# Modulation panels moved from mixer to feed-forward, silu by pairs, two squares summed by TensorE

## The chip, the cores and the metric

The kernel runs on one core of a Trainium2 chip. The metric is the device time of one execution in microseconds, the median of several runs. The engines are named as the profile names them: PE is TensorE (PEld its weight loads), DVE is VectorE, ACT is ScalarE, POOL is GpSimd, SP is SyncE, which issues the DMAs of the weights.

## What is computed

Two models follow each other on x, 256 tokens of width 1024 in fp32. The first is one layer of a delta rule and attention; the change touches it only in its norms. The second has two layers, and each of them is feed-forward, mixer, feed-forward. Every one of these has a norm in front that is modulated by a vector c: nine rows of 1024 per layer, each a product of silu(c) with 1024 columns of w_mod.

```python
for l in range(DEPTH_2):
    mod = silu(c) @ w_mod[l] + b_mod[l]
    sh1, sc1, g1, sh2, sc2, g2, sh3, sc3, g3 = split(mod[:, None, :], N_MOD)
    h = _rmsnorm_2(x) * (1.0 + sc1) + sh1
    x = x + HALF_STEP * g1 * _swiglu(h, ffn1_w_gate[l], ffn1_w_up[l], ffn1_w_down[l])
    h = _rmsnorm_2(x) * (1.0 + sc2) + sh2
    x = x + g2 * _hybrid_mixer(h, w_in[l], w_out[l], ...)
    h = _rmsnorm_2(x) * (1.0 + sc3) + sh3
    x = x + HALF_STEP * g3 * _swiglu(h, ffn2_w_gate[l], ffn2_w_up[l], ffn2_w_down[l])

def _swiglu(h, w_gate, w_up, w_down):            # 1024 -> 2816 -> 1024
    return (silu(h @ w_gate) * (h @ w_up)) @ w_down

def _hybrid_mixer(h, ...):                       # 28 panels of 128 columns of w_in
    qa, ka, va, qd, kd, vd, qh, fh, ih, gh = split(h @ w_in)
    o_a = stick_breaking(qa, ka, va)
    o_d = dilated_mixture(rope(norm(qd)), rope(norm(kd)), vd)
    o_h = hgrn2(silu(qh), gates(fh), ih)
    o_h = _rmsnorm_2(o_h) * hgrn_norm_g * silu(gh)
    return concat(o_a, o_d, o_h) @ w_out
```

## The kernel before

**Numbers.** All products are in fp32 by three matmuls: each operand is split into a rounded half H and a rest L, and L*H, H*H and H*L are added up (`mm3`). Weights come in panels of 128x1024. `wload` (L94) brings one: SP issues its DMA into a `raw` buffer (seven of them), ACT casts it to `wh` (L98), DVE subtracts to get `wl` (L99); of `wh` and `wl` there are four each. "Split" below means these two steps. Activations lie transposed, 128 channels by 256 tokens (T) in eight tiles (KD = 8).

**Stages.** First block to 372 us, feed-forward of layer 0 to 561, mixer to 716, feed-forward to 904, then layer 1 the same way: to 1092, 1247 and 1436. A feed-forward first runs 22 pairs f of a gate and an up panel (tiles `psf`, `psu`; 48 matmuls a pair), then eight panels m of the down matrix (`psd`).

**Order.** Code is written in the order of the mathematics; a scheduler then sets one fixed order for each engine's queue, by its own estimates of when things are ready. An engine works its queue strictly in that order.

**Norms.** `stat(k)` (L142) makes, for each eighth k of x, the scaled halves `xH` (ACT L152) and `xL` (DVE L153) and the square `sq` (ACT L155). The squares 1 to 6 are added to the first one, `sqa`, by POOL (L157, `tensor_add` on `seng`; by DVE in the first block's first two norms); the eighth, `sql`, is kept apart. `stat_close` (L160) has PE sum both over channels by a matmul with ones (`pss` L165, two matmuls for each tile, one for each half of the tokens), DVE adds the epsilon (`nms` L168), POOL takes the power (`nr` L170), PE spreads the result (`rb` L173). There are eight such norms. So that PE needn't wait for it, the first panels behind a norm are multiplied with the unnormed x (`pre`, L187: four panels in a mixer, five pairs in a feed-forward) and scaled afterwards; `norm` (L200) makes in the meantime the normed `hH` and `hL` (L206, L207) for the rest.

**Panels.** The modulation rows are computed by DVE: a panel of w_mod is loaded by SP, multiplied with silu(c) and summed by one instruction (L744, two records: the operation and the read of its sum). There are 8 panels to a row, 144 for both layers and 8 for the first block. `pump(n)` lets n of them run at that place of the program, `need(last)` drains what a stage's vector still lacks. `pump(1)` stands behind each f from `NPRE` on and behind seven of the eight m, and in the mixer behind each of the four dilated projections; `need(last)` stands at the end of the gate and up pairs, and in the mixer ahead of the output projection.

**Mixer.** Projections `pT` (one panel each, tile `psp`) and `ptok` (two panels, `pst`). After the four `pre` panels (gate f, `hsg`, `hk`, `hf`) come four for q (`hqt` by ACT L295, `hq` by DVE L296, from which the levels of the gated recurrence start: `RK`, `hs`), and so on. Interleaved generators make the stick-breaking part (`pv`), the dilated part (`nk`, `dk1a` on DVE L431, `dk1r` by POOL L432, `rp` L1204, `rsu`, `rke`, `rkb` L444; `ds`, `de`) and the recurrence (`hov`, sums of its squares `hjk` on ACT, `hra` DVE L431, `hrr` POOL L432, `hon` DVE L578, transposed by PE as `hot` L586, times the gate `hG` as `hy` L589, split as `yH`, `yL`). `hG` is the silu of four projections (L684); ACT keeps one set of function tables, and a change of set shows as ACT_TABLE_LOAD. Then come the output projections (`pso`) and `update`, which calls `stat` for the next norm.

## Time and profile before

| | us |
|---|---|
| median of 3 runs | 1442.99 (1441.73 to 1444.32) |
| the profiled execution, its own time | 1442.31 |
| its span, first to last instruction | 1440.5 |
| PE busy | 1403.3 (97%) |
| PEld busy | 1305.3 (91%) |
| DVE busy | 1141.0 (79%) |
| ACT busy | 771.0 (54%) |
| POOL busy | 85.7 (6%) |

Busy time is the union of an engine's instructions. Matmuls overlap: one of 256 columns is recorded with 0.28 us, but in a full stretch one starts every 0.12 us, so a wait is best read from the starts, or from the idle time in brackets behind a row, which names what ended it. "x4" behind a row counts records that follow each other; a pair of matmuls for `pss` leaves four. PEclk is the granted clock of TensorE, 1.00 for 2.4 GHz and 0.50 for 1.2 GHz.

### The profile page before, as it was taken

Reading aid. Unit: us, or ns where it says so; the run is one execution under the profiler, and the core shown is the slowest. Engines: PE = TensorE matmul, PEld = TensorE weight load, DVE = VectorE, ACT = ScalarE, POOL = GpSimd, SP = SyncE. Lnnn points to the kernel's source line nnn. Section 1 sums busy time; section 2 is a strip of 40 time slices with the busy share of each in tenths; the row PEclk is TensorE's granted clock in tenths of the full one; section 3 lists DMA queues with packets and bytes.
Section 4 is the critical chain, followed back from the end, with each engine's and each line's share of the span. In section 5 each row is a group of like instructions: output and inputs, shape, how many; then the busy total and the mean of one; then the engine's idle time right before and its main releaser. Section 6 shows DMA issues by size and latency. Waiting matters only on the chain. (4 is left out here: it accounts for less than half of the span.)

```text
span 1440.5 us, 27393 instructions
## 1 busy us (share of the span) xinstructions
PE 1403.3 (97%) x10786; PEld 1305.3 (91%) x10786; DVE 1141.0 (79%) x2124; ACT 771.0 (54%) x1315; POOL 85.7 (6%) x87
## 2 busy tenths in 40 slices
PE   7999989999999999999999999999999999999998
PEld 4798867889999989998899998999989998899997
DVE  6769888858887887888897797977688889796554
ACT  4654586644644446447564444544446357554442
POOL 0011100012100001001100001000011010100000
PEclk9999999999999999999999999999999999999999
DMA  8524545635688985557568897688774557577562
GB/s 317 195 64 124 150 147 174 222 103 164 198 288 276 323 286 182 176 153 252 171 202 303 271 356 243 201 283 286 237 255 158 172 175 234 175 242 241 172 199 70
DMA packets 94833, 303.98 MB, mean 211 GB/s; under 512 B 18128, under 2 KB 20432, under 8 KB 94448
## 3 DMA queue, kind: packets, MB, share of 16 engines
q1 hardware_dynamic: 89824, 299.90, 63.3%
q8 instruction: 85, 1.39, 0.4%
q10 hardware_dynamic: 4432, 1.11, 0.4%
q0 software_dynamic: 448, 1.21, 0.3%
q14 instruction: 44, 0.36, 0.1%
HBM read 300.09 MB, written 2.10 MB: 210 GB/s over the span
## 5 line engine op out<-in xcount | busy, mean ns | idle before, releaser
L98 ACT CAST wh<-raw 128x1024 fp32r<-128x1024 f32 (+3 forms) x407 | 414.6, 1021 | 288.2 <-PE psd L121 89.1
L99 DVE TENSOR_TENSOR wl<-raw,wh 128x1024 fp32r<-128x1024 f32 (+3 forms) x407 | 481.5, 1187 | 94.5 <-ACT wh L98 93.6
L111 PE MATMUL psf<-hH,wh 128*128 128x256 f32 x1088 | 306.1, 281 | 0.0
L112 PE MATMUL psf<-hL,wh 128*128 128x256 f32 x1088 | 305.6, 281 | 0.0
L110 PE MATMUL psf<-hH,wl 128*128 128x256 f32 x1088 | 305.4, 281 | 0.0
L121 PE MATMUL psd<-gHL,wh 128*128 128x512 f32 x704 | 244.3, 392 | 0.0
L744 DVE CUSTOM_DVE_ANT_0 raw<-raw,mrow 128x1024 f32<-128x1024 f32 x152 | 184.5, 1219 | 69.7 <-DMA raw<-in_wmod 68.1
L110 PEld LDWEIGHTS psf<-hH,wl 128*128 128x128 f32 x1088 | 205.6, 189 | 0.0
L112 PEld LDWEIGHTS psf<-hL,wh 128*128 128x128 f32 x1088 | 205.5, 189 | 0.0
L111 PEld LDWEIGHTS psf<-hH,wh 128*128 128x128 f32 x1088 | 204.8, 188 | 0.0
L122 PE MATMUL psd<-gHL,wl 128*128 128x256 f32 x704 | 196.8, 280 | 0.0
L121 PEld LDWEIGHTS psd<-gHL,wh 128*128 128x128 f32 x704 | 132.2, 188 | 29.0
L110 PE MATMUL psp<-hH,wl 128*128 128x256 f32 x512 | 149.6, 292 | 2.4 <-DVE wl L99 2.4
L111 PE MATMUL psp<-hH,wh 128*128 128x256 f32 x512 | 148.2, 289 | 0.0
L112 PE MATMUL psp<-hL,wh 128*128 128x256 f32 x512 | 147.0, 287 | 0.0
L122 PEld LDWEIGHTS psd<-gHL,wl 128*128 128x128 f32 x704 | 132.2, 188 | 0.0
L110 PEld LDWEIGHTS psp<-hH,wl 128*128 128x128 f32 x512 | 97.7, 191 | 5.5 <-PE psp L112 1.7
L112 PEld LDWEIGHTS psp<-hL,wh 128*128 128x128 f32 x512 | 97.7, 191 | 1.6 <-issue 1.0
L111 PEld LDWEIGHTS psp<-hH,wh 128*128 128x128 f32 x512 | 97.3, 190 | 1.2 <-issue 0.7
L249 ACT ACTIVATE ft<-psf 128x256 f32<-128x256 f32 x68 | 26.2, 386 | 112.2 <-PE psf L112 112.2
L157 POOL TENSOR_TENSOR sqa<-sqa,sq 128x256 f32<-128x256 f32 x36 | 31.3, 868 | 593.9 <-issue 481.3
L252 ACT CAST gHL<-ft 128x256 fp32r<-128x256 f32 x88 | 35.7, 406 | 28.1 <-DVE ft L250 22.3
(513 smaller groups left out, 2789.3 us busy)
## 6 DMA issues: line engine op xcount, KB each, us to landing
raw<-in_ffn_gu SPq DMA_DIRECT2D x176, 512.0 KB, 4.4
raw<-in_wmod SPq DMA_DIRECT2D x144, 512.0 KB, 4.5
raw<-in_ffn_dn SPq DMA_DIRECT2D x64, 448.0 KB, 4.1
raw<-in_win SPq DMA_DIRECT2D x56, 512.0 KB, 4.3
raw<-in_w_rest SPq DMA_DIRECT2D x32, 512.0 KB, 3.8
raw<-in_ffn_dn SPq DMA_DIRECT2D x32, 512.0 KB, 4.6
raw<-in_wmod_sc SPq DMA_DIRECT2D x12, 512.0 KB, 7.4
raw<-in_wout_a SPq DMA_DIRECT2D x16, 384.0 KB, 4.0
```

Of the source, the lines that this page charges most:

```text
L98: nc.scalar.copy(H[:, :n], raw[:, :n])
L99: nc.vector.tensor_sub(L[:, :n], raw[:, :n], H[:, :n].bitcast(F32))
L110: mm(ps, L[:, s], hH[:, b, :T], start=f, stop=False)
L111: mm(ps, H[:, s], hH[:, b, :T], start=False, stop=False)
L112: mm(ps, H[:, s], hL[:, b, :T], start=False, stop=l)
L121: mm(ps, H[:, s], h[:, b, :, :T], start=first and i == 0, stop=False)
L122: mm(ps[:, 1, :], L[:, s], h[:, b, 0, :T], start=False, stop=last and i == len(kw) - 1)
L157: self.seng.tensor_add(self.sqa, self.sqa, o)
L249: nc.scalar.activation(t, ps[:, 0, :], AF.Silu)
L252: nc.scalar.copy(gH[:, f, :], t)
L744: nc.vector.tensor_tensor_reduce(raw, raw, row, op0=ALU.mult, op1=ALU.add, scale=1.0, scalar=0.0, accum_out=t[:, j : j + 1])
```

## The change

1. `stat` and `stat_close`: the seventh square isn't added to `sqa` any more; both last squares stay apart, and PE sums three tiles instead of two.
2. `norm` takes a function that it calls ahead of its third and seventh step; the mixer gives it a `wload` of the next panel, and the first two `pT` behind it take these. The first four `wload` of a mixer stand ahead of its loop.
3. The four `pump(1)` of the mixer go; the feed-forward pumps two panels behind every third f and every second m.
4. The gate's projections are copied, and Silu runs once on each pair, 128x512.

```diff
-        if 0 < k < KD - 1:
+        if 0 < k < KD - 2:
             self.seng.tensor_add(self.sqa, self.sqa, o)
-        self.sql = o
+        elif k:
+            self.sql.append(o)
+        else:
+            self.sql = [o]
...
-        for i, a in enumerate((self.sqa, self.sql)):
+        for i, a in enumerate(self.sql):
             for t in range(2):
                 nc.tensor.matmul(pss[:, t : t + 1], a[:, t * P : (t + 1) * P], self.ones,
-                                 start=i == 0 and t == 0, stop=i == 1, skip_group_check=True)
+                                 start=i == 0 and t == 0, stop=i == 2, skip_group_check=True)
...
-    def norm(self, sh, into):
+    def norm(self, sh, into, between=None):
...
         for k in range(KD):
+            if between and k % 4 == 2:
+                between()
...
-                    self.pump(1)
+                    self.pump(1 + (f % 3 == 0))
...
-                self.pump(1 if m < 7 else 0)
+                self.pump(1 + m % 2 if m < 7 else 0)
...
-        self.mm3(ps[:, 0, :], self.wload(src), h, range(KD), range(KD), True, True)
+        self.mm3(ps[:, 0, :], src if isinstance(src, tuple) else self.wload(src), h, range(KD), range(KD), True, True)
...
-            pT = lambda: self.projT(win[next(u)], h)
+            Ws = [self.wload(win[next(u)]) for _ in range(4)]
+            ahead = []
+            pT = lambda: self.projT(win[next(u)] if not ahead else ahead.pop(0), h)
...
-                cz = self.pre(ps, self.wload(win[next(u)]))
+                cz = self.pre(ps, Ws[i])
...
-                    h = self.norm(sh, 0)
+                    h = self.norm(sh, 0, lambda: ahead.append(self.wload(win[next(u)])))
...
                 self.dil_q(pool, C, pT(), j, self.gq[:, l : l + 1], dz, nq)
                 next(st)
-                self.pump(1)
...
                 self.dil_k(pool, C, pT(), j, self.gk[:, l : l + 1], dT)
                 next(st)
-                self.pump(1)
...
-                nc.scalar.activation(G[:, i, :], z, AF.Silu)
+                nc.scalar.copy(G[:, i, :], z)
+                if i % 2:
+                    nc.scalar.activation(G[:, i - 1 : i + 1, :], G[:, i - 1 : i + 1, :], AF.Silu)
```

The lines of the kernel shift by 4 to 10 with the change (L99 stays, L157 becomes L161, L744 becomes L752). Three places show how the order of the engines moves.

DVE at the start of the first mixer, before: the eight steps of `hL`, then the split of the second `pT`'s panel, and the third's ahead of the second `hq`.

```order
L207 SCALAR_TENSOR_TENSOR hL_6557<-xs_6558,mod2_0_100,hH_6556 128x256 x8
L197 COPY cs_6449<-psp_6625 128x1
L640 TENSOR_TENSOR hsg_6659<-psp_6625,rbs_6462 128x256
L638 TENSOR_SCALAR hnz_6657<-cs_6449 128x1
L99 TENSOR_TENSOR wl_6703<-raw_6700,wh_6702 128x1024
L645 TENSOR_SCALAR hf_6464<-hsg_6619,lbq_4212 128x256
L296 SCALAR_TENSOR_TENSOR hq_6466<-hqt_6696,psp_6665 128x256
L645 TENSOR_SCALAR hf_6464<-hsg_6659,lbq_4212 128x256
L545 COPY RK_6863<-hf_6464 128x512
L522 TENSOR_TENSOR RK_6863<-hk_6465,RK_6863 128x256x2
L99 TENSOR_TENSOR wl_6737<-raw_6734,wh_6736 128x1024
L296 SCALAR_TENSOR_TENSOR hq_6466<-hqt_6730,psp_6699 128x256
```

After, behind the first six steps of `hL`: the split, two more steps, and the third panel's split behind the second `hq`.

```order
L201 COPY cs_6462<-psp_6658 128x1
L648 TENSOR_TENSOR hsg_6686<-psp_6658,rbs_6477 128x256
L646 TENSOR_SCALAR hnz_6684<-cs_6462 128x1
L99 TENSOR_TENSOR wl_6613<-raw_6610,wh_6612 128x1024
L213 SCALAR_TENSOR_TENSOR hL_6584<-xs_6585,mod2_0_100,hH_6583 128x256 x2
L653 TENSOR_SCALAR hf_6479<-hsg_6652,lbq_4213 128x256
L653 TENSOR_SCALAR hf_6479<-hsg_6686,lbq_4213 128x256
L302 SCALAR_TENSOR_TENSOR hq_6481<-hqt_6717,psp_6692 128x256
L551 COPY RK_6878<-hf_6479 128x512
L528 TENSOR_TENSOR RK_6878<-hk_6480,RK_6878 128x256x2
L302 SCALAR_TENSOR_TENSOR hq_6481<-hqt_6745,psp_6720 128x256
L99 TENSOR_TENSOR wl_6752<-raw_6749,wh_6751 128x1024
```

The third panel's `wl` has changed places with the second `hq`; two `hL` stand behind the second panel's `wl`.

DVE in the middle of the first mixer, from the first `dT` to the row behind `dk1a`, before: `dqa`, for which POOL then takes the power `dqr`, stands here, and so does DVE's use of `dqr`.

```order
L1207 TENSOR_TENSOR dT_6472<-rsu_7416 128x256
L431 TENSOR_SCALAR dqa_7623<-nq_6473 128x8
L744 ISA raw_7863,mcol_7355<-raw_7863,mrow_415 128x1024
L744 ISA mcol_7355 128x1
L446 TENSOR_TENSOR dT_6472<-dT_6472,rkb_7423 128x256
L451 TENSOR_SCALAR dqr_7624<-dqr_7624 128x8
L744 ISA raw_7866,mcol_7355<-raw_7866,mrow_415 128x1024
L744 ISA mcol_7355 128x1
L387 SCALAR_TENSOR_TENSOR sa_7433<-sa_7433 128x384
L387 SCALAR_TENSOR_TENSOR sa_7436<-sa_7436 128x384
L431 TENSOR_SCALAR dk1a_7496<-nk_7493 128x4
```

After, the same stretch: one panel is left in it, and `dqa` and `dqr` are gone from it (`dqa` now stands ten rows ahead of `dk0a`, `dqr` right behind that).

```order
L1215 TENSOR_TENSOR dT_6487<-rsu_7423 128x256
L752 ISA raw_7872,mcol_6308<-raw_7872,mrow_417 128x1024
L752 ISA mcol_6308 128x1
L452 TENSOR_TENSOR dT_6487<-dT_6487,rkb_7430 128x256
L393 SCALAR_TENSOR_TENSOR sa_7440<-sa_7440 128x384
L393 SCALAR_TENSOR_TENSOR sa_7443<-sa_7443 128x384
L437 TENSOR_SCALAR dk1a_7500<-nk_7497 128x4
```

Ahead of `dk1a` stand one panel and the two `dqa`, `dqr` rows fewer.

PE from the end of the first mixer to the feed-forward, before: the sum of `sqa`, then three matmuls on, that of the last square.

```order
L165 MATMUL pss_8263<-ones_88,sqa_8153 128x1 x2
L194 MATMUL psf_8277<-xL_8155,wh_8280 128x258
L194 MATMUL psf_8277<-xH_8154,wl_8281 128x258
L194 MATMUL psf_8277<-xH_8154,wh_8280 128x258
L165 MATMUL pss_8263<-ones_88,sq_8255 128x1 x2
L194 MATMUL psu_8291<-xH_8154,wh_8286 128x258
L194 MATMUL psf_8277<-xL_8155,wh_8280 128x258
L194 MATMUL psf_8277<-xH_8154,wl_8281 128x258
L194 MATMUL psf_8277<-xH_8154,wh_8280 128x258
L194 MATMUL psf_8277<-xL_8155,wh_8280 128x258
L194 MATMUL psu_8291<-xL_8155,wh_8286 128x258
L173 MATMUL rb_8272<-ident_86,nr_8270 128x128 x2
```

After, from the second of three sums on (the first one stands twelve matmuls ahead of it):

```order
L169 MATMUL pss_8268<-ones_88,sq_8256 128x1 x2
L198 MATMUL psf_8284<-xL_8161,wh_8287 128x258
L198 MATMUL psf_8284<-xH_8160,wl_8288 128x258
L198 MATMUL psf_8284<-xH_8160,wh_8287 128x258
L198 MATMUL psf_8284<-xL_8161,wh_8287 128x258
L198 MATMUL psf_8284<-xH_8160,wl_8288 128x258
L169 MATMUL pss_8268<-ones_88,sq_8260 128x1 x2
L198 MATMUL psf_8284<-xH_8160,wh_8287 128x258
L198 MATMUL psu_8298<-xH_8160,wh_8293 128x258
L198 MATMUL psf_8284<-xL_8161,wh_8287 128x258
L198 MATMUL psf_8284<-xH_8160,wl_8288 128x258
L198 MATMUL psf_8284<-xH_8160,wh_8287 128x258
```

The first sum has moved ahead by 15 matmuls of the feed-forward, the one of the seventh square is new, and `rb` follows the last sum at about the same distance.

## Rows read from the trace of the kernel before

**Rows 1.** The page's engines: busy us, share of the span, instructions

```profile
PE 1403.3 (97%) x10786; PEld 1305.3 (91%) x10786; DVE 1141.0 (79%) x2124; ACT 771.0 (54%) x1315; POOL 85.7 (6%) x87
```

**Rows 2.** Windows of feed-forward and mixer: engines, PEclk, DMA share, GB/s

```profile
400.00:500.00 100.00, 100.00 (x842) 100.00 (x841) 81.56 (x126) 47.59 (x71) 0.00 (x0) 1.00 0.85 295
...
561.00:716.00 155.00, 149.35 (x1207) 140.90 (x1206) 132.97 (x270) 90.75 (x156) 14.14 (x12) 1.00 0.57 185
```

**Rows 3.** PE's list of waits, whole span: us in total, times, longest

```profile
PE hot L586 <- DVE hon L578: 1.9, 2, 1.0
```

**Rows 4.** PE's timeline, first mixer's start: start, us; idle before in brackets

```profile
577.66 0.36 PE L110 MATMUL psp<-hH,wl 128*128 128x256 f32 x1 [0.65 <-DVE wl L99]
...
581.75 0.38 PE L110 MATMUL psp<-hH,wl 128*128 128x256 f32 x1 [0.56 <-DVE wl L99]
```

**Rows 5.** DVE's timeline of the same place

```profile
580.48 1.22 DVE L99 TENSOR_TENSOR wl<-raw,wh 128x1024 fp32r<-128x1024 f32 x1
581.62 0.41 DVE L296 SCALAR_TENSOR_TENSOR hq<-hqt,psp 128x256 f32<-128x256 f32 x1
```

**Rows 6.** PE's timeline, first mixer's middle

```profile
655.27 0.67 PE L1204 MATMUL rp<-rsu,Cdperm 128*128 128x256 f32 x2 [0.45 <-DVE dk1a L431]
...
657.84 0.71 PE L444 MATMUL rkb<-ident,rke 128*128 128x128 f32 x4 [0.73 <-DVE rsu L1205]
```

**Rows 7.** DVE's and POOL's timelines of the same place

```profile
652.81 0.17 DVE L451 TENSOR_SCALAR dqr<-dqr 128x8 f32<-128x8 f32 x1 [1.19 <-POOL dqr L432]
652.89 1.22 DVE L744 CUSTOM_DVE_ANT_0 raw<-raw,mrow 128x1024 f32<-128x1024 f32 x1
...
654.98 0.15 DVE L431 TENSOR_SCALAR dk1a<-nk 128x4 f32<-128x4 f32 x1
...
655.21 1.92 POOL L432 TENSOR_TENSOR dk1r<-dk1a,negh 128x4 f32<-128x4 f32 x1 [2.43 <-DVE dk1a L431]
```

**Rows 8.** PE's timeline, first mixer's tail

```profile
684.13 0.33 PE L586 MATMUL hot<-ident,hon 128*128 128x128 f32 x1 [0.96 <-DVE hon L578]
...
689.52 0.38 PE L110 MATMUL pso<-yH,wl 128*128 128x256 f32 x1 [0.34 <-ACT yH L289]
...
690.64 0.39 PE L112 MATMUL pso<-yL,wh 128*128 128x256 f32 x1 [0.39 <-DVE yL L290]
```

**Rows 9.** Window ahead of that tail, and DVE's row behind it

```profile
665.00:680.00 15.00, 15.00 (x130) 14.03 (x130) 15.00 (x43) 13.10 (x28) 0.00 (x0) 1.00 0.89 309
...
681.47 0.17 DVE L431 TENSOR_SCALAR hra<-hss 128x8 f32<-128x8 f32 x1 [0.15 <-ACT hjk L574]
```

**Rows 10.** ACT's table loads for the gate's silu

```profile
L684 ACT ACT_TABLE_LOAD x6 | 7.7, 1283 | 0.1
```

**Rows 11.** PE at the mixer's head and behind it; POOL's adds (page)

```profile
560.98 0.50 PE L165 MATMUL pss<-ones,sqa 128*128 128x1 f32 x4
561.34 0.37 PE L194 MATMUL psp<-xH,wl 128*128 128x258 f32 x1
...
719.34 0.61 PE L165 MATMUL pss<-ones,sqa 128*128 128x1 f32 x4 [0.72 <-POOL sqa L157]
...
L157 POOL TENSOR_TENSOR sqa<-sqa,sq 128x256 f32<-128x256 f32 x36 | 31.3, 868 | 593.9 <-issue 481.3
```

**Rows 12.** Panels: first mixer, then feed-forward

```profile
L744 DVE CUSTOM_DVE_ANT_0 raw<-raw,mrow x17: 1203/1216/1223, 598.4 to 677.2; 128x1024 f32<-128x1024 f32 x17
L744 DVE DVE_READ_ACCUMULATOR2_ANT mcol<- x17: 78/81/93, 599.5 to 678.4; 128x1 f32 x17
...
L744 DVE CUSTOM_DVE_ANT_0 raw<-raw,mrow 128x1024 f32<-128x1024 f32 x24 | 29.2, 1221 | 9.4 <-DMA raw<-in_wmod 9.4
```

**Rows 13.** Windows behind first and second mixer's end

```profile
723.00:725.00 2.00, 2.00 (x19) 2.00 (x19) 2.00 (x5) 1.73 (x2) 0.00 (x0) 1.00 0.10 20
1254.00:1256.00 2.00, 2.00 (x12) 2.00 (x11) 1.55 (x4) 1.14 (x2) 0.00 (x0) 0.50 0.22 16
```

**Rows 14.** The page's transfers in 40 slices

```profile
GB/s 317 195 64 124 150 147 174 222 103 164 198 288 276 323 286 182 176 153 252 171 202 303 271 356 243 201 283 286 237 255 158 172 175 234 175 242 241 172 199 70
```

## The prediction, as it was put on record

> **What bounds the kernel now.** I read the busy shares first, then the windows by stage, then PE's list of waits, and last the timelines around each wait. PE is busy for 97% of the span, and no other engine is close [rows 1]. In the feed-forward PE is busy for all of 100 us and issues 842 matmuls, one every 0.119 us [rows 2]: nothing on another engine can shorten that stage, it can only be harmed. In the mixer PE is busy 149.35 of 155 us [rows 2]. So what this change can win is PE's idle time in two mixers and at the norms, about 6 us each, and only where the moved work ends such a wait. The list of waits names them; the costliest that touch this change are hot on hon, psp on wl, and pss on the sums of squares [rows 3, 4, 11]. The second layer's mixer repeats the first's waits (hot has two, both alike, [rows 3]), so the rows are of the first and count twice.
>
> The sum is made against the profiled execution, 1442.31 us (span 1440.5), which is 0.7 us under the median of 1442.99; I apply the difference to the median.
>
> **Panels.** One panel costs DVE 1.22 us and a read of 0.08, 1.30 together [rows 12]. By the rule that what was not pumped is drained where the vector is needed, 17 panels stand in either mixer before [rows 12]; counted through the new pumps it is 14 in the first mixer and 5 in the second. DVE is thus freed of 3.9 and 15.6 us. None of that is on PE's path by itself: it counts only where DVE is what PE waits for.
>
> *Middle.* PE waits 0.45 us for rp and 0.73 for rkb [rows 6]. Behind both is dk1a on DVE at 654.98, queued behind a panel (652.89) and behind dqr, for which DVE stood 1.19 us waiting on POOL [rows 7]. In the new order dqa stands ten rows ahead of dk0a, so dqr is there before DVE comes to it, and dk1a no longer has that wait ahead of it. DVE could have it 1.2 us earlier. Then PE's own nk is late next: nk now stands 5 matmuls ahead of rp and rkb 11 behind it, 16 matmuls or 1.9 us and rp itself, which is about 0.2 us short of what POOL's power (1.92, [rows 7]) and the copies around it need. 1.18 less 0.18 gives **-1.0 us in each mixer** (0 to -1.2).
>
> *Tail.* DVE is busy for 15.00 of the 15 us up to 680 and ACT for 13.10 [rows 9]; hra follows at 681.47 [rows 9], and PE then waits 0.96 us for hot, 0.34 for yH and 0.39 for yL, 1.69 in all [rows 8]. In the second mixer only one panel stands between dT and hra, where some eleven stood, so hra loses up to 13 us of DVE work ahead of it and is bound by ACT and PE; PE's order has it transpose hon all four at once with 24 projection matmuls (2.9 us) behind it before ds. I take all 1.69, and 0.3 for two of the three refills (a first matmul behind a wait lasts about 0.1 longer than its neighbours): **-2.0 us** (-1.0 to -2.3). In the first mixer ten panels still stand ahead of hra, so DVE stays full there; it gains one split fewer ahead of hra and ACT's shorter chain. I take half of 1.69: **-0.85 us** (0 to -1.7).
>
> **Gate by pairs.** A table load is 1.28 us [rows 10]; loads fall from 11 to 7 in a mixer, 5.1 us of ACT, all near the tail, where ACT is 87% busy [rows 9]. The copies cost about what the four activations did. No wait of PE names hG, so this is worth only what it lets hov's squares, and with them hra, come earlier; that is in the tail's number, and nothing is added. A rule speaks against the pair: the Trainium skill, in "Perfetto Trace Analysis", section "Optimizing Scalar/DVE Operations", says that where ACT and DVE are not saturated but cause bubbles on others, breaking instructions up lets work finish sooner. Here both are nearly full just there [rows 9], so by the trace the condition isn't met; by the rule the pair would make hy later and the tail's 0.85 would shrink to nothing.
>
> **First weights ahead.** The first four splits stood in this order already, and only the two between the norm's steps are new: two hL now stand behind the second projection's split. PE waits 0.65 us for that split and 0.56 for the next [rows 4]. The first should fall to about 0.25. But the next split, which DVE started at 580.48 ahead of hq [rows 5], now stands behind hq, which itself needs the end of that projection and ACT's copy. That puts it at about 581.2, its end at 582.4, and PE's start 0.65 later than 581.75 [rows 4], with two more hs done meanwhile (0.3). Net **+0.3 us in each mixer** (-1.2 if nothing holds the split, +1.0 if the hs bring nothing and hL is late too).
>
> **Squares.** POOL loses one add of 0.87 us per norm [rows 11], PE gets a third pair of matmuls. A pair stands for 0.36 us on PE (560.98 to 561.34, [rows 11]). There are eight norms. At the heads of two mixers and of the second layer's first feed-forward PE didn't wait for the sum (the row at 560.98 has no idle before it), so it is **+0.36 us three times**. From mixer to feed-forward PE waited 0.72 [rows 11]; with the last add gone the sum is 1.1 us earlier, but PE's order puts that pair 15 matmuls earlier too, where it still waits about 0.5, and the short wait at rb behind it is covered: **-0.25 us twice** with the third pair paid (-0.7 to +0.4). From the first block to its feed-forward it is about +0.1. In the first block's head PE waits for other things at both norms; I take 0 (-0.5 to +0.7).
>
> **Feed-forward.** The panels' DMAs move with them, from a stage with a DMA share of 0.57 into one with 0.85 [rows 2]; SP issues win's panels in the order it had. The extra panels take DVE from 82% to 89% of the stage: one more per three pairs, which last 3 x 48 x 0.119 = 17.1 us. PE has no wait there, and I cost it at nothing. DVE's idle time is the cover; what happens when it is gone is the second rival.
>
> **Sum.** First mixer -1.0 - 0.85 + 0.3 + 0.36 - 0.25 = -1.4; second -1.0 - 2.0 + 0.3 + 0.36 - 0.25 = -2.6; the two other norms +0.5; first block 0. Together -3.5: 1438.8 for an execution such as the profiled one, **1439.5** as a median.
>
> **The clock.** At 1254 to 1256 the granted clock is 0.50 (1.2 GHz), and PE issued 12 matmuls where the first mixer's like stretch at full clock has 19 [rows 13]. That is some 0.8 us there, about 1.5 with the neighbouring slices. The work before it was the same in both layers. The Trainium skill, "TensorE: Matmul & The Clock Gate", section "What's actually happening", has the array at half clock by default and released by recent activity; by it, fewer waits should keep the drop away. The trace agrees that it comes behind waits, but the first layer had the same waits and no drop. I leave it out of the sum and in the range.
>
> **Rivals.** *Given back, no change (0.31).* The scheduler's new order hands out what the panels gave: rkb waits for nk, hra in the first mixer stays where it was behind ten panels, and hq holds the split for the whole +1.0. Then it is -0.5 in the first mixer's middle and tail, -1.5 in the second's, +2.0 at the two starts, +0.7 for the two mixers' head pairs, -0.5 behind them, +0.5 for the others: +0.7 or, with half of the start, -0.3, so 1442 to 1443.5. For it: DVE's order, which I can read; against: dqr's wait is plainly gone.
>
> *Slower: the feed-forward becomes DVE's (0.07).* DVE stood 9.4 us at 24 panels in 100 us, 0.39 each [rows 12]. At 89% busy its idle time is 1.85 us in 17.1, so four panels may wait 0.46 each; beyond that DVE runs late and PE stops at wl. At 0.60 it would be 0.56 us per 17.1, 4 us in a gate-and-up stage, 12 in the three that get more panels: 1451. The transfers would go from 295 GB/s at a share of 0.85 [rows 2] to 326 at 0.94. Against it: one slice of the page, 36 us in a feed-forward, moved 356 GB/s [rows 14] with PE full, and a wait of an engine that is early shrinks as it gets busier.
>
> *More (0.14).* The split isn't held (-1.2 instead of +0.3 in both mixers), or the first tail's waits go too (another -0.85) and the clock stays at 1.00 (-1.5): 1435.5 to 1437.2.
>
> *The panels don't leave the first mixer* is not a rival but a fact of the order, 14 of 17 stay; where a reader expects half the gain from there, it is missing.
>
> **How the numbers follow.** My forecast has 0.48, from about 1437.5 to 1441 by the bounds of middle, tail and start. About 0.2% is what a measurement of this kernel can tell from no change: below 1440.1 and above 1445.9. Of the forecast's 0.48, 0.43 lie below 1440.1, and all of "more"; that is 0.57 faster, 0.36 same, 0.07 slower. The range leaves out the slower rival, the upper part of "given back" and the lowest of "more": 1435.8 to 1443.2.
>
> **What would show it.** Right: no idle before rp, under 0.3 before rkb; in the second mixer's tail no idle before hot; the third projection's first matmul later by about 0.3 than before, counted from the second's start of norm; twelve records of pss in a norm instead of eight, 0.36 us more where PE doesn't wait; PE 100% in the feed-forward with DVE at 88 to 90%. Wrong: a wait on wl or on a panel in the feed-forward, a new drop of the granted clock, or hra unmoved in the second mixer.

## The result

The changed kernel takes 1461.96 us (median; 1460.51 to 1466.68) against 1443.47: a ratio of 1.0140, interval 1.0119 to 1.0161. It is slower by 18.5 us. The forecast was 1439.5 with a range to 1443.2, so the direction was wrong. What happened is the rival that had 0.07: in the feed-forward PE came to wait for DVE. A smaller loss, in the first block, was in none of the cases.

The page's engines of the changed kernel, as [rows 1], whose shares hardly move:

```profile
PE 1412.4 (97%) x10818; PEld 1309.5 (90%) x10818; DVE 1134.8 (78%) x2122; ACT 756.0 (52%) x1311; POOL 81.2 (6%) x81
```

The table is worked out from the traces: a stage lasts from PE's first matmul into `psf` or `psd`, or out of them into the mixer's tiles, to the next such matmul (the feed-forward's first matmuls that stand among a mixer's last ones count to the mixer). "gu" is a gate-and-up stage, "dn" the down stage behind it; 1.0 is the first feed-forward of layer 0, 2.0 the second, 1.1 and 2.1 those of layer 1. The kernels e1 to e20 are the experiments below.

```
            block1  gu1.0  dn1.0   mix0  gu2.0  dn2.0  gu1.1  dn1.1   mix1  gu2.1
before      372.99 126.98  61.38 155.09 126.35  61.38 126.69  61.38 155.13 127.88
after       377.00 132.37  64.60 155.63 126.69  62.95 131.48  64.46 151.89 126.37
e1 panels   373.31 132.66  63.56 154.31 126.82  64.16 132.11  62.85 154.89 126.35
e2 no pan.  379.42 126.83  61.83 156.72 126.34  61.83 126.84  63.32 155.62 126.38
e3 squares  379.54 126.85  61.83 155.25 126.33  61.83 126.83  61.83 155.29 126.37
e5          377.44 126.83  61.83 158.61 126.38  61.83 126.84  62.80 159.87 126.35
e6          377.94 128.97  62.44 153.48 129.53  63.66 128.84  62.96 151.71 126.35
e7          407.72 128.78  61.83 157.94 126.36  61.83 126.83  61.83 151.52 126.36
e12         372.58 131.15  64.04 154.83 127.47  63.47 131.95  62.90 151.77 126.33
e13         372.04 128.78  64.64 152.54 126.33  62.97 130.58  62.15 151.77 126.33
e14         377.51 127.05  61.83 155.39 126.38  61.83 126.81  63.27 155.06 126.38
e15         371.56 127.19  61.38 156.20 126.35  61.38 126.70  61.39 156.40 127.79
e16         371.39 127.18  61.38 154.85 126.96  64.37 126.71  62.16 154.70 126.34
e17         371.64 127.05  61.83 155.22 126.38  61.83 126.82  61.83 155.34 126.37
e20         372.80 127.19  61.38 152.52 128.36  61.38 126.70  61.91 152.80 126.34
```

After less before: first block +4.0; the three feed-forwards that got doubled pumps +8.6, +1.9 and +7.9; first mixer +0.5, second -3.2; the last gate-and-up stage -1.5.

PE's list of waits in the changed kernel has two lines that before has not, both in the feed-forward:

```profile
PE psf L110 <- DVE ft L256: 6.5, 5, 1.9
...
PE psd L122 <- DVE wl L99: 4.5, 6, 1.4
```

A window of 100 us of the first feed-forward, and one of the second mixer, as [rows 2]; the columns are PE, PEld, DVE, ACT and POOL busy, PEclk, DMA share, GB/s:

```profile
400.00:500.00 100.00, 97.38 (x813) 96.76 (x813) 78.95 (x125) 43.98 (x67) 0.00 (x0) 1.00 0.85 289
1115.00:1267.00 152.00, 147.66 (x1207) 140.66 (x1208) 120.13 (x245) 86.58 (x154) 13.89 (x13) 1.00 0.47 147
```

PE issues 813 matmuls where it issued 842, and DVE is less busy than before (78.95 against 81.56), not more. The panels' row for the same 100 us, as the last of [rows 12], tells why:

```profile
L752 DVE CUSTOM_DVE_ANT_0 raw<-raw,mrow 128x1024 f32<-128x1024 f32 x24 | 29.3, 1221 | 19.5 <-DMA raw<-in_wmod 19.5
```

As many panels, 24, of the same 1221 ns; but DVE stood 19.5 us waiting for their transfers instead of 9.4. One such wait in full, first SP's issue of the panel, then DVE from the panel before it on, then PE:

```profile
496.74 0.33 SPq L90 DMA_DIRECT2D raw<-in_wmod  x1
```

```profile
495.49 1.22 DVE L752 CUSTOM_DVE_ANT_0 raw<-raw,mrow 128x1024 f32<-128x1024 f32 x1
496.63 0.08 DVE L752 DVE_READ_ACCUMULATOR2_ANT mcol<- 128x1 f32 x1
...
498.18 1.22 DVE L99 TENSOR_TENSOR wl<-raw,wh 128x1024 fp32r<-128x1024 f32 x1
501.92 1.23 DVE L752 CUSTOM_DVE_ANT_0 raw<-raw,mrow 128x1024 f32<-128x1024 f32 x1 [2.52 <-DMA raw<-in_wmod]
503.07 0.08 DVE L752 DVE_READ_ACCUMULATOR2_ANT mcol<- 128x1 f32 x1
503.07 0.42 DVE L256 TENSOR_TENSOR ft<-ft,psf 128x256 f32<-128x256 f32 x1
```

```profile
503.54 0.39 PE L110 MATMUL psf<-hH,wl 128*128 128x256 f32 x1 [1.93 <-DVE ft L256]
```

DVE has read the sum of the panel before at 496.71 (496.63 and 0.08); the next panel's transfer is issued at 496.74, right behind that. DVE comes to it at 499.4 and stands until 501.92. Behind it in DVE's queue is `ft`, which empties a buffer of `psf`; PE stands 1.93 us for that buffer and starts 0.05 after `ft` ends. It is the rival's chain, a late DVE, but for its end: the rival had PE stop at `wl`, and in this stage PE stops at `ft`.

### The profile page after: what moved, and what is told of

Its sections match the earlier page's. It is cut to its first block, busy times and chain, and to the rows that moved or that the text cites. A ratio compares the mean times of both kernels' runs of the same rounds, so it can differ in the third digit from the quotient of the medians.

```text
span 1458.7 us, 27446 instructions
## 1 busy us (share of the span) xinstructions
PE 1412.4 (97%) x10818; PEld 1309.5 (90%) x10818; DVE 1134.8 (78%) x2122; ACT 756.0 (52%) x1311; POOL 81.2 (6%) x81
## 5 line engine op out<-in xcount | busy, mean ns | idle before, releaser
L99 DVE TENSOR_TENSOR wl<-raw,wh 128x1024 fp32r<-128x1024 f32 (+3 forms) x407 | 481.2, 1186 | 86.4 <-ACT wh L98 85.3
L752 DVE CUSTOM_DVE_ANT_0 raw<-raw,mrow 128x1024 f32<-128x1024 f32 x152 | 185.2, 1220 | 91.1 <-DMA raw<-in_wmod 89.6
L152 ACT ACTIVATE xH<-xT,mod 128x256 fp32r<-128x256 f32 x48 | 24.4, 508 | 77.8 <-DVE xT L219 77.4
```

The lines of the kernel that those rows point to most:

```text
L99: nc.vector.tensor_sub(L[:, :n], raw[:, :n], H[:, :n].bitcast(F32))
L152: nc.scalar.activation(H, x, AF.Copy, scale=s)
L752: nc.vector.tensor_tensor_reduce(raw, raw, row, op0=ALU.mult, op1=ALU.add, scale=1.0, scalar=0.0, accum_out=t[:, j : j + 1])
```

## The experiments

### Which edit: panels alone, everything but the panels, mixer's pumps away alone

e1 is the kernel before with

```diff
-                    self.pump(1)
+                    self.pump(1 + (f % 3 == 0))
-                self.pump(1 if m < 7 else 0)
+                self.pump(1 + m % 2 if m < 7 else 0)
-                self.pump(1)     # behind dil_q and behind dil_k
```

> The kernel before with the change's pumps alone (none in the mixer, two behind every third f and every second m); squares, norm and gate as before. DVE's order in the first feed-forward is then that of the changed kernel. Theory A (a panel whose transfer is late stands in DVE's queue ahead of ft and wl, and PE stops behind it; the pumps alone bring that order): the three feed-forwards with double pumps lose about what they lost in the changed kernel, +8.7, +1.9 and +7.9 us, the second mixer gains about 3, the first block stays at 373 us: 1455 to 1460. Theory B (the third pair of sums or the other edits disturb the feed-forward): near 1440. The first block's +4 us is from the sum of squares by both.

Measured 1458.96 (ratio 1.0119, 1.0103 to 1.0135). PE's list of waits of e1 has the same two lines:

```profile
PE psf L110 <- DVE ft L250: 6.7, 7, 1.4
...
PE psd L122 <- DVE wl L99: 4.1, 5, 1.2
```

Feed-forwards +18.0 in sum, the first block at 373.3. So the pumps alone bring the feed-forward's loss. The second mixer missed: 154.89, though it holds 5 panels as in the changed kernel.

e2 is the changed kernel with these lines put back.

> The changed kernel with all pumps as before: squares, weights ahead and gate by pairs stay. Theory A: no wait of PE on ft or wl in the feed-forwards, whose lengths are those of before (127 and 61 us); the first block is 4 us longer as in the changed kernel, the mixers lose or gain under 2 us: 1443 to 1448. Theory B: the feed-forwards still lose over 10 us in sum, 1455 or more.

Measured 1450.65 (1.0061, 1.0043 to 1.0079), a little above the range: the first block lost 6.4 and not 4, the first mixer 1.6, and the down stages 2.8 in sum. All gate-and-up stages are those of before.

e5 puts back the feed-forward's two lines only.

> The changed kernel with the feed-forward's pumps as before; the mixer's four pumps stay away, so its panels are drained ahead of the output projection. Theory A: the feed-forwards are those of before; the first block +4, mixers near those of the kernel without the panels' edit, 1440 to 1448. If leaving the pumps out of the mixer is what harms (its drain at the end), a mixer is longer by over 2 us than with pumps.

Measured 1455.33 (1.0090, 1.0071 to 1.0109), above the range: the mixers take 158.6 and 159.9, where e2 with its pumps takes 156.7 and 155.6. PE waits 9.3 us there for the output projection's `wl`: what is not pumped is drained by `need(last)` ahead of those splits on DVE, all 17 at once. So pumps may leave the mixer only as far as panels leave it.

### What about them: DVE's work, the transfer, the ring, or the place

e7 leaves the transfers out and keeps the work:

```diff
-            raw = self.wraw(src, 1024)
-            nc.vector.tensor_tensor_reduce(raw, raw, row, ...)
+            raw = self.stand                  # one standing buffer; weights keep six
+            nc.vector.tensor_tensor_reduce(raw, row, row, ...)
```

> The changed kernel with the panels' transfers left out: DVE runs the panel's instruction as often and for as long, on data that stand in its memory (the modulation is then not that of the reference), and the weights keep six raw buffers. Theory A (DVE's instructions fit; the late transfer ahead of ft and wl is what stops PE): no wait of PE on ft or wl in the feed-forwards, which take 127 and 61 to 62 us; with the first block's 4 and the second mixer's gain 1440 to 1445. Theory A2 (the instructions themselves are too many for DVE where two stand together): PE's waits on ft stay, the three feed-forwards lose over 10 us in sum: 1453 or more.

The total (1478.53, 1.0250, 1.0218 to 1.0281) is far above the theory's range and says nothing here: with nothing to wait for, the scheduler put 78 panels into the first block, which grew to 407.7 us. But its first feed-forward then holds 44 panels where the others hold 25, and 22 in its down stage. The windows of both, and the panels' row of the first:

```profile
408.00:536.00 128.00, 126.57 (x1060) 126.16 (x1059) 126.28 (x221) 65.18 (x99) 1.64 (x1) 1.00 0.59 178
536.00:598.00 62.00, 62.00 (x364) 54.69 (x362) 61.97 (x96) 29.69 (x41) 3.97 (x6) 1.00 0.60 182
```

```profile
L754 DVE CUSTOM_DVE_ANT_0 praw<-mrow 128x1024 f32<-128x1024 f32 x44 | 55.1, 1253 | 0.0
```

Forty-four panels without a wait cost that stage 1.8 us: DVE is busy 126.28 of 128, so it is just the bound, and 22 in the down stage cost nothing beside the third sum (61.83 is also e3's). The scheduler placed them, more than two to a pair where the pumps stand. In the changed kernel 25 with late transfers cost 5.4. DVE's work is not what was too much.

e6 halves the transfers: every second panel reuses the buffer of the one ahead of it.

```diff
-            raw = self.wraw(src, 1024)
+            if j % 2 == 0:
+                raw = self.wraw(src, 1024)
```

> The changed kernel, but every second panel is not loaded: the instruction runs a second time on the buffer of the panel before it, so DVE does the same work with half the panels' transfers and buffers (the modulation is then made from half of its columns). Theory A1 (what is late is the transfer, because the panel takes a place in the ring of seven raw buffers and is issued only when a slot comes free): PE's waits on ft and wl in the feed-forward go, the three feed-forwards come back to within 1 us of before in sum: 1441 to 1447 with the first block's 4 us. Theory A2 (DVE itself is overloaded where two panels stand together, 2 x 1.30 us ahead of ft): they stay, over 10 us: 1455 or more.

Measured 1453.40 (1.0075, 1.0047 to 1.0103), between the two. Window and panels' row of the first feed-forward:

```profile
400.00:500.00 100.00, 98.36 (x823) 97.95 (x822) 80.50 (x130) 45.44 (x69) 0.00 (x0) 1.00 0.73 237
```

```profile
L753 DVE CUSTOM_DVE_ANT_0 raw<-raw,mrow 128x1024 f32<-128x1024 f32 x25 | 30.6, 1222 | 17.7 <-DMA raw<-in_wmod 17.7
```

Moving 237 instead of 289 GB/s DVE still waits 17.7 us, on half as many transfers. So it isn't the traffic that makes a panel late. My A1 said that halving would do; it did only in part (128.97 us for this stage, and 129.53 for the second one). I read it so that a panel that stands early in DVE's queue waits for its own transfer however few others there are; no run tests that alone.

e8 gives the panels two raw buffers of their own and the weights five (`wraw(src, 1024, "praw", 2)`).

> The changed kernel with two raw buffers for the panels alone and five for the weights, seven in all as before. If the panels are late because they share one ring with the weights (a panel's transfer can be issued only when the load seven places before it has been split), the panels' waits on DVE fall to under half (89.6 us before) and the three feed-forwards come back to within 4 us in sum: 1442 to 1450. If they are late because DVE's order puts the panel ahead of weights that SP issues first, its waits stay near 90 us and so does the loss of 18: 1455 to 1465.

Measured 1491.39 (1.0358, 1.0320 to 1.0396), outside both: with five buffers the first block alone takes 403.8 us and the first mixer 169.3. Whether a larger ring would cure the lateness stays open; none was tried.

e14 is the changed kernel with the gate-and-up loop's pump as before; the down stage keeps its doubled pumps.

```diff
-                    self.pump(1 + (f % 3 == 0))
+                    self.pump(1)
```

> The changed kernel with one pump behind every f as before; the down phase keeps two behind every second m, the mixer none. The gate-and-up stages then hold as many panels as before and as after (24 to 25 in the first, drained at its end), only their places differ. Theory (two panels side by side in DVE's queue, with late transfers, stop PE; not their number in the stage): the first gate-and-up stage takes 126.8 instead of 132.4 us, the down stages still lose 1.5 to 3 each: 1446 to 1454, more where the mixer has to drain what the feed-forward did not take. Rival (their number decides): 132 us in the first gate-and-up stage.

Measured 1448.55 (1.0038, 1.0023 to 1.0054), as the theory had it, but the down stages lose less than it said (0.45, 0.45 and 1.9): most of what they lose in the changed kernel also comes from the doubled pumps ahead of them. Windows of the first feed-forward's two stages, and the panels' row as above:

```profile
377.50:504.50 127.00, 127.00 (x1066) 127.00 (x1066) 104.03 (x177) 65.43 (x99) 0.72 (x1) 1.00 0.79 268
504.50:566.50 62.00, 62.00 (x363) 54.70 (x363) 51.97 (x71) 30.88 (x41) 5.09 (x6) 1.00 0.89 300
```

```profile
L752 DVE CUSTOM_DVE_ANT_0 raw<-raw,mrow 128x1024 f32<-128x1024 f32 x23 | 28.0, 1222 | 18.8 <-DMA raw<-in_wmod 18.8
```

PE stands nowhere, with 25 panels in the stage as in both other kernels and 9 in the down stage as in the changed one. DVE waits 18.8 us for transfers here too, almost as long as in the changed kernel. So neither the number of panels nor the sum of the waits decides. e3 (below), whose pumps are those of before, says the same: its stage takes 126.85 us with this row, where before's waits are 9.4 in all:

```profile
L747 DVE CUSTOM_DVE_ANT_0 raw<-raw,mrow 128x1024 f32<-128x1024 f32 x24 | 29.2, 1224 | 19.9 <-DMA raw<-in_wmod 19.9
```

What decides is the place together with the waits: late transfers cost nothing behind single pumps (e14, e3), and work side by side costs little without transfers (e7). A sum that fits is that of one pair's 5.7 us. By the starts of e14's rows (441.30 to 445.47), a pair with one panel is 4.2 us of DVE's work (two splits, a panel and two small operations), which leaves 1.5 for a wait, and e14's waits are 1.0 to 1.8; with two it is 5.4, which leaves 0.3, and what a wait takes beyond that goes to PE. This is an estimate: taken over three pairs (13.8 of 17.1 us, 0.8 left for each of four panels) it fits as well, and no run tells the two apart. In before and in e14 the panels that are left over are drained at the end of the stage, when the pairs' own weights have landed.

### Squares

e3 is the kernel before with the change to `stat` and `stat_close` alone.

> The kernel before with the change to the squares alone. Theory (the four to six us that the first block lost come from its head, where the third pair of sums and two squares kept apart reorder PE and DVE and the clock falls at 20 to 40 us): the first block takes 377 to 379 us instead of 373, the granted clock is under 1.00 between 20 and 40 us, each mixer's and the second layer's head 0.4 us longer: 1446 to 1450. Rival (the first block's loss comes from the gate, the norm or chance): first block at 373, 1442 to 1444.

Measured 1447.79 (1.0044, 1.0028 to 1.0060). PE's rows in the first block's head, before and then e3:

```profile
28.14 2.32 PE L967 MATMUL psm<-raw,cc 128*2 128x256 f32 x10
31.99 0.58 PE L165 MATMUL pss<-ones,sqa 128*128 128x1 f32 x4 [1.53 <-DVE sqa L157]
```

```profile
28.65 0.59 PE L970 MATMUL psm<-raw,cc 128*2 128x256 f32 x2
31.02 0.58 PE L168 MATMUL pss<-ones,sqa 128*128 128x1 f32 x4 [1.78 <-DVE sqa L157]
...
31.97 0.59 PE L970 MATMUL psm<-raw,cc 128*2 128x256 f32 x2
32.50 0.95 PE L168 MATMUL pss<-ones,sq 128*128 128x1 f32 x4
33.38 1.87 PE L970 MATMUL psm<-raw,cc 128*2 128x256 f32 x4
```

Before, ten matmuls of the first modulation (`psm`) stand ahead of the second norm's sum; now two do, and the rest wait behind sums and `rb` for DVE's squares. Their raw buffers come free later: from 24 to 48 us SP waits 19.3 us for `psm` in e3, 13.2 in before, and the DMA share at 36 to 40 falls from 0.93 to 0.56, in these windows of before and of e3 (the last three columns are PEclk, DMA share, GB/s):

```profile
32.00:36.00 4.00, 4.00 (x24) 2.32 (x25) 2.81 (x8) 0.56 (x2) 1.26 (x2) 1.00 0.88 264
36.00:40.00 4.00, 4.00 (x21) 1.57 (x20) 3.17 (x9) 3.86 (x10) 0.02 (x1) 1.00 0.93 358
```

```profile
32.00:36.00 4.00, 3.85 (x14) 1.88 (x14) 1.31 (x5) 0.00 (x0) 1.61 (x1) 0.57 0.83 246
36.00:40.00 4.00, 4.00 (x13) 1.42 (x13) 2.55 (x5) 1.22 (x3) 0.40 (x1) 0.57 0.56 158
```

The clock falls too, to 0.57, and that has a price of its own: 12 matmuls of `psm` take 4.15 us, where before 18 take 4.05, some 1.4 us by that rate (an estimate).

```profile
35.71 4.05 PE L967 MATMUL psm<-raw,cc 128*2 128x256 f32 x18
```

```profile
36.54 4.15 PE L970 MATMUL psm<-raw,cc 128*2 128x256 f32 x12
```

How much of the head's loss is the clock and how much the order was not separated. A smaller drop need not cost in the end: e12, the changed kernel without the squares, has one in these windows, is 1.4 us late at `psb`'s first matmul (44.3 us in before; e3 is 4.3 late there), and its first block still takes 372.6 us.

```profile
32.00:36.00 4.00, 4.00 (x20) 2.25 (x20) 2.15 (x7) 0.36 (x1) 1.28 (x2) 0.75 0.89 256
36.00:40.00 4.00, 4.00 (x18) 1.52 (x17) 3.34 (x9) 2.98 (x7) 0.00 (x0) 0.82 0.67 256
```

> The changed kernel with the squares as before. Theory (squares cost the first block 4 to 6 us and each norm 0.36 where PE doesn't wait; panels cost the feed-forwards 18): the first block is back at 373, the feed-forwards stay slow (132, 64, 127, 63, 131, 64), the second mixer stays at 152: 1454 to 1458, some 5 us under the changed kernel. Rival (the first block's loss comes with any reordering): it stays at 377 or more, 1459 to 1463.

e12 measured 1456.19 (1.0095, 1.0065 to 1.0125): 4.4 us of first block back, the rest 2.5 us shorter in sum than in the changed kernel.

e17 keeps the two sums in the head's norms (`0 < k < KD - 1 - (self.seng is nc.gpsimd)`), three in the six others.

> The kernel before with three sums only in the six norms behind the first block's head, two in its two norms as before. Theory (the squares' loss is the head's: the third sums stand among the modulation matmuls there and hold their raw buffers): first block at 373, heads of mixers and feed-forward longer by 0.4 each, the two norms behind the mixers shorter by 0.3: within 1 us of before, 1441.5 to 1443.5. Rival (the sums cost at every norm): 1445 or more.

Measured 1442.48 (1.0001, 0.9993 to 1.0010). The first block is at 371.6, so its loss comes with the third sums in the head's two norms. The total hides a loss, though: each of the three heads behind a down stage is 0.45 us longer (61.83, also in e3), the two mixers 0.1 and 0.2, and the norms behind the mixers give nothing back. The last gate-and-up stage makes up for it, 126.37 us instead of 127.88 by a clock drop that is gone (see the clock, below), and so does the first block, 1.35 shorter than before's in this execution for no reason that the rows show. Of e3's 6.5 us in the first block, 4.3 are there at 44 us; a further 2.9 come between 196 and 204, where its granted clock is 0.55 to 0.59. The changed kernel has the first part alone.

### Gate by pairs

e10 is the kernel before with the four lines of the gate.

> The kernel before with the gate by pairs alone. Theory (the table loads stand in ACT's chain to hov's squares and hra): hra some 1 us earlier and PE's wait for hot shorter by 0.3 to 1 in each mixer, 1440.5 to 1442 against 1442. Rival (the silu of the second pair comes later than the single ones, and hy and yH with it): mixers 0 to 1.5 us longer, PE waits on yH instead of hot, 1442 to 1445.

Measured 1441.58 (0.9997, 0.9984 to 1.0011): nothing. Table loads fall from 11 to 9 in a mixer; the changed kernel has 7, so this run tests only part of what the edit does there. PE's waits:

```profile
PE pso L110 <- ACT yH L289: 2.2, 2, 1.1
...
PE hot L586 <- DVE hon L578: 1.7, 2, 0.9
```

Hot is waited for 0.2 us less in sum than in [rows 3], `yH` 1.5 us more (0.7 before). The mixers are within 0.1 of before. Both readings are seen in part, and neither moves the total.

### A version that is faster

e13 is e12 with each panel's load written one pump ahead of its use:

```diff
-            raw = self.wraw(src, 1024)
+            raw = self.wraw(src, 1024) if j == 0 else nxt
+            if j < len(srcs) - 1:
+                nxt = self.wraw(srcs[j + 1], 1024)
```

> The kernel before this one in the list (the change without the squares) with each panel's load written one pump ahead of its use, so that a panel holds a raw buffer longer and its transfer can be issued some 4 us earlier. Theory (the transfers are issued 2 to 4 us before DVE is free for them and take 4.5; that lateness is what the doubled pumps turn into PE's waits): DVE's waits for panels in the first feed-forward fall from 22.0 and 11.9 us to under half, its stages to 128 and 62.5 us, the whole to 1440 to 1447. Rival (the ring of seven is full, so a panel that is loaded earlier only makes the weights late): waits of DVE move from panels to ACT's wh, PE's loss stays over 10 us: 1452 to 1460.

Measured 1448.67 (1.0038, 1.0025 to 1.0051), 7.5 under e12: a third of the feed-forward's loss goes and the first mixer falls to 152.5. That is a little above the theory's range, and DVE's waits in the first gate-and-up stage fell to 15.4 us, not to under half; the pairs still stand side by side.

e16 takes out the squares and doubles a gate-and-up stage's pumps only in the second feed-forward of layer 0 (`nf` counts them), where that stage had lost 0.3; the down stages keep two panels behind every second m.

```diff
-                    self.pump(1 + (f % 3 == 0))
+                    self.pump(1 + (f % 3 == 0 and self.nf == 1))
```

> The change without the squares, and with two panels behind every third f only in the first layer's second feed-forward, where the changed kernel lost 0.3 us by them; one behind each f in the others; the mixer none. Theory (loss by place, not by number): first block 373, the two first feed-forwards' gate-and-up stages 127, down stages 61.5 to 63, second mixer 152 as in the changed kernel: 3 to 5 us of mixer and clock kept, 1438.5 to 1442 against 1442.4. Rival (what the feed-forward takes more it always gives back, wherever it stands): second feed-forward and second layer's first lose 3 or more: 1443 to 1448.

Measured 1446.28 (1.0026, 1.0013 to 1.0039), the rival's range: gu2.0 and the down stage behind it lose 3.6. So doubling isn't free in this gate-and-up stage either; what the stage itself hides, DVE brings late into the down stage. e18 is e16 with the loads ahead.

> The first kernel of this list with each panel's load written one pump ahead of its use. Theory (single panels with earlier transfers leave DVE without waits, and the mixers drain faster): first mixer 152.5 to 153.5 as with this load before, feed-forwards as in the first of the list: 1436 to 1440. Rival (a raw buffer held longer makes weights late): feed-forwards lose 2 or more each, 1442 to 1447.

Measured 1442.37 (0.9998, 0.9985 to 1.0011): no difference from before, above the theory's range. e20 has single pumps in all gate-and-up stages, loads ahead, and no squares; e15 has the loads ahead alone, on the kernel before.

> The change without the squares and with one panel behind each f in every feed-forward (two behind every second m stay, none in the mixer), each panel's load written one pump ahead. Theory (two side by side in a gate-and-up stage are what costs, there and in the down stage behind it): every gate-and-up stage within 0.5 us of before, down stages 61.4 to 62.5, first mixer 152.5 to 153.5: 1437 to 1441. Rival (any panel more in a feed-forward costs): down stages 63 to 64.5, 1442 to 1446.

> The kernel before with nothing but each panel's load written one pump ahead of its use. If the shorter first mixer (152.5 instead of 155.1) seen with such loads comes from them alone: mixers 152.5 to 153.5, feed-forwards as before, 1437 to 1440. If it comes from the mixer without pumps: mixers at 155, 1441 to 1444.

e20 measured 1439.65, a ratio of 0.9984 (0.9971 to 0.9996): its interval just leaves out no change, and it is 22 us under the changed kernel. Its windows of the first feed-forward:

```profile
373.00:500.00 127.00, 127.00 (x1065) 126.92 (x1065) 103.66 (x175) 64.55 (x99) 0.72 (x1) 1.00 0.79 267
500.00:561.00 61.00, 61.00 (x354) 53.71 (x353) 52.41 (x73) 30.23 (x41) 5.83 (x6) 1.00 0.88 311
```

PE doesn't stand, with 11 panels in the down stage instead of 6, and the mixers take 152.5 and 152.8. e15 measured 1445.51 (1.0023, 1.0013 to 1.0033), above both of its cases, mixers at 156. The loads ahead shorten a mixer only together with the mixer's other edits (no pumps, weights ahead, gate by pairs); which of these they need was not tried. Nor were single pumps without loads ahead and without the squares.

Single runs of a kernel lie some 8 us apart here (before: 1438.9 to 1447.1; e16: 1442.1 to 1450.6), and the table has one execution of each; a stage in it can hold a drop of the clock, as e20's gu2.0 does (0.62 granted from 720 to 724 us). The totals go by medians and intervals.

## Why the prediction was wrong

**Feed-forward, costed at nothing; +18.4 us.** The step that failed is "PE has no wait there, and I cost it at nothing", with DVE's idle time as the cover and the reason that "a wait of an engine that is early shrinks as it gets busier". It did not shrink: 0.39 us a panel before, 0.81 in the changed kernel's window. The rows above show why it need not. A panel's load waits for DVE itself: it is issued 0.03 us behind the read of the panel ahead, which ends at 496.71. So it is in e14: the read is done at 442.53, the next load is issued at 442.56, and DVE stands 1.43 us for it until 446.90. A DVE that comes late to one panel gets the next one late as well. The growth of the waits alone was not the loss, though: e3 waits about as long and loses nothing. It took two panels in one pair, and with them the wait, ahead of `ft` and `wl`.

The count failed too. "One more per three pairs" would have made DVE 89% busy. By my own rule a stage drains at its end what it has not pumped, so the first gate-and-up stage held 25 panels before and holds 25 after (in layer 1 it is 19 and 25); only their places moved, and DVE's share fell to 79%. For the same reason the rival's threshold of 0.46 us a panel was too low. Its 82% counts the drain; where the pumps stand DVE was less busy:

```profile
407.00:477.00 70.00, 70.00 (x590) 70.00 (x589) 53.32 (x77) 32.53 (x48) 0.00 (x0) 1.00 0.83 282
411.00:481.00 70.00, 68.31 (x572) 67.91 (x571) 52.59 (x81) 30.80 (x47) 0.00 (x0) 1.00 0.86 294
```

These are before and the changed kernel, with 13 and 17 panels. Four more panels on 53.32 us would leave some 0.7 us for each of 17 (an estimate); they waited 16.5 us, 0.97 each. So the rival was right in kind, and its formula, which gives 10 us a stage at 0.81, too steep: 5.4 was measured. I also took traffic as the case against it (356 GB/s in a slice); e6 shows that halving the panels' traffic does not end the waits. The chance of 0.07 came from those sentences, and the row that spoke against them, 9.4 us of DVE's waits on DMA, was in front of me.

**First block, 0; +4.0** (e3: +6.5). I bounded the squares there by +0.7, since PE waits in that head anyway. That looked at PE's waits and not at what stands behind the sums in PE's queue: matmuls that free raw buffers. The clock's drop in the head, which the bound left out as well, has a part in it that was not separated.

**Middle, -1.0 in each mixer; about 0.** The rows of the changed kernel that answer to [rows 6] are both of rkb, and POOL's stands behind the first:

```profile
662.42 0.68 PE L450 MATMUL rkb<-ident,rke 128*128 128x128 f32 x4 [0.65 <-DVE rke L446]
...
670.07 0.71 PE L450 MATMUL rkb<-ident,rke 128*128 128x128 f32 x4 [0.48 <-DVE rsu L1213]
```

```profile
659.96 1.99 POOL L438 TENSOR_TENSOR dk0r<-dk0a,negh 128x4 f32<-128x4 f32 x1 [4.87 <-DVE dqr L457]
```

The wait at rp is gone, as said, and the second rkb waits 0.48 instead of 0.73 (I had left it 0.18). But the first rkb, which had none, now waits 0.65: POOL's power for `dk0a` takes 1.99 us, where it took 1.01 before, and DVE stands 0.89 for its result. Why the same operation took twice as long no row shows. The waits sum to 1.18 before and 1.13 after. I followed dk1a and not the chain ahead of it.

**Tail, first mixer -0.85; worse.** The rows that answer to [rows 8]:

```profile
691.46 0.33 PE L490 MATMUL dpt<-ident,de 128*128 128x128 f32 x1 [0.96 <-DVE de L487]
...
696.97 0.33 PE L592 MATMUL hot<-ident,hon 128*128 128x128 f32 x1 [0.70 <-DVE hon L584]
```

Hot waits 0.70 instead of 0.96, `yH` and `yL` about as before, and a new wait of 0.96 for `de` stands ahead of them. **Second mixer -2.0; right in kind.** No wait for hot is left there, and hra waits for ACT and no longer for panels:

```profile
1229.39 0.17 DVE L437 TENSOR_SCALAR hra<-hss 128x8 f32<-128x8 f32 x1 [2.05 <-ACT hjk L580]
```

The whole second mixer gained 3.2 where the sum gave 2.6 for it and the norm behind it. By e1 (154.9 with as few panels), e2 and e10 (no gain without panels moved) it takes the panels' leaving together with the mixer's other edits; which of these was not tried.

**Start, +0.3 in each mixer; about right.** PE's waits for psp on wl fell from 2.4 to 1.5 us over the span, and a new one for hs on hq has 1.0. **Later norms, +0.7 in sum; too low.** In e17 and e3 the three heads cost 0.45 us each, near the 0.36 forecast, but the norms behind the mixers, priced at -0.25 each, gave nothing back, and the mixers are 0.1 to 0.2 longer. By its trace, e17's equal total comes from the clock and the first block.

**Gate by pairs, nothing by itself; right** by e10, as far as the total goes. The Trainium skill ("Perfetto Trace Analysis", section "Optimizing Scalar/DVE Operations") says that where ACT and DVE aren't saturated but cause bubbles on others, breaking instructions up may let work finish sooner. e10's wait for `yH`, 2.2 us instead of 0.7, goes its way, though both were nearly full there in before [rows 9]; the wait for hot went the other way.

**The clock, left out; it gave 1.5.** The drop behind the second mixer is gone in the changed kernel and in all experiments but e10 and e15, whose last gate-and-up stage still takes 127.8 to 127.9. The stretch behind the second mixer, as [rows 13]:

```profile
1273.00:1275.00 2.00, 2.00 (x19) 2.00 (x18) 1.64 (x4) 1.69 (x4) 0.00 (x0) 1.00 0.00 0
```

The gate-and-up stage is 126.37 instead of 127.88, the 1.5 us that I had priced for the range. That fewer waits keep the drop away isn't shown: e1 stands as long as before in the stretch ahead of it and has no drop. These are before and e1, two stretches each, from 2.0 and from 6.0 us behind the mixer's end:

```profile
1249.37:1251.37 2.00, 1.29 (x12) 1.09 (x10) 1.53 (x3) 0.43 (x2) 0.85 (x1) 1.00 0.38 76
1253.37:1255.37 2.00, 2.00 (x11) 2.00 (x11) 1.48 (x3) 0.72 (x3) 0.00 (x0) 0.50 0.00 0
```

```profile
1266.67:1268.67 2.00, 1.28 (x12) 1.09 (x10) 1.54 (x3) 0.44 (x2) 0.86 (x1) 1.00 0.35 53
1270.67:1272.67 2.00, 2.00 (x19) 2.00 (x18) 1.86 (x4) 1.64 (x4) 0.00 (x0) 1.00 0.00 0
```

What did keep it away stays open.

**The sums.** They come out as written, but for the low end of "more": 1439.5 less the 3.0 of two splits is 1436.5, not 1435.5.

## What to carry to other kernels

An engine that waits in a fixed queue is not idle time to be filled: ask what stands behind the waiting instruction, what releases the transfer that it waits for, and whether work and wait together fit into the time that the pacing engine gives. Before counting what a move adds to a stage, count what that stage already holds by the rule that drains the rest. And where one edit moves work and three others reorder it, run each alone: here the squares and the gate alone were worth nothing or less, and the only kernel with moved panels that came out faster, by 0.16%, has single pumps in the gate-and-up stages and earlier loads.

## What the runs showed of the hardware

At 36 to 40 us e3's PE is recorded as busy for all of 4.00 us, and its granted clock is 0.57: 13 matmuls started there, where before started 21 at full clock. The 0.57 is a mean over the window of the two levels, 1.2 and 2.4 GHz. What brought the clock down isn't shown: PE stood 1.78 us for `sqa` ahead of it, and in before 1.53 us without a drop.

A panel's load took as long from issue to landing, in the median, with a fifth less traffic (237 instead of 289 GB/s in the windows above). The page's rows of transfers (count, KB each, median us from issue to landing), of the changed kernel and of e6 with half of the panels' loads:

```profile
raw<-in_wmod SPq DMA_DIRECT2D x144, 512.0 KB, 4.5
```

```profile
raw<-in_wmod SPq DMA_DIRECT2D x72, 512.0 KB, 4.5
```

The median is 4.5 us in both, as in the kernel before; single loads of the changed kernel's first gate-and-up stage took 3.5 to 6.4. So whether a panel is late was here mostly a matter of when its load was issued.
